# Down-projection of a squared-ReLU MLP: a chunk's seven products chained in PSUM, context products as plain float32

## The chip, the cores and the metric

One core of one Trainium2 chip runs the whole program: two layers of a hybrid backbone on 1,024 latent positions and 256 context positions. TensorE (PE in the profile) multiplies out of SBUF into PSUM, which has eight banks of 128 partitions by 512 float32. VectorE (DVE), ScalarE (ACT) and GpSimd (POOL) do the elementwise work, and SyncE (SP) issues most transfers from and to DRAM. Each engine runs its own instructions in the order of its own queue and waits for the others at semaphores. The metric is the device time of the program in microseconds.

## The reference, cut to what matters

Three token mixers run side by side in each layer, their outputs are projected and added, and then the MLP follows. The change lies in the second product of that MLP, the down-projection.

```python
def sqrelu_mlp(h, w_up, w_down):
    return jnp.square(jax.nn.relu(h @ w_up)) @ w_down

for l in range(DEPTH):                       # DEPTH = 2
    ...
    x = x + ga2 * sqrelu_mlp(modulate(rmsnorm(x, g_norm2[l]), sh2, sc2), w_up[l], w_down[l])
    if not last:                             # the context is needed after layer 0 only
        xc = xc + ga2c * sqrelu_mlp(modulate(rmsnorm(xc, g_norm2[l]), sh2c, sc2c), w_up[l], w_down[l])
return rmsnorm(x, g_final)
```

`x` is 1024 x 1024 in float32, the hidden width is 4096, and `xc` has 256 rows.

## The kernel before

**Number form.** A float32 product is made of three products in the reduced form f32r. Each operand tile is split: ScalarE casts it to its high half (line 142), VectorE or POOL subtracts that from the tile to get the low half (line 143), and `mm3` multiplies high by high, high by low and low by high into one bank (lines 133, 138, 139). Which of the two engines makes a low half is set by a pattern that is stepped through call by call (`lo_`): `DL = "GV"` alternates POOL (G) and VectorE (V) for the down-projection.

**Blocks.** The 1024 positions are two blocks, xT[0] and xT[1], the context is block 2. The up-projection has written the squared ReLU to DRAM as four quadrants (`da`: A11, A12, A21, A22) and for the context as `dac` (layer 0 only). Here the hidden axis is cut into four chunks (`for c in range(NCH)`). Per chunk, four quadrants of A and four of the weight (B11 to B22) come in by `load`, sixteen transfers of 512 KB on SP's queue. Eight combinations of quadrants (`comb`, line 1449) are two 128x1024 operations each, spread over VectorE and POOL by `DA = "GVVV"`. Then come seven block products, P1 to P7, in place of the eight that a plain 2 x 2 multiplication has.

**A product.** `run` (line 1451) goes over four tiles of 128 hidden units. It splits one A and one B tile each and issues `mm3` on four banks: 4 x 4 x 3 = 48 TensorE instructions of 128x512. Split tiles live in a ring of four for A and four or five for B. The eight PSUM banks are six of a pool called "mm" and two of "t"; a product takes four banks, the next one the others.

**After a product.** `put` (line 1416) adds gain x source to the residual tile on VectorE, 128x512 (128x256 for the context); in the last chunk it also squares the new value on ScalarE and adds it to the norm's sum `ss` on POOL or VectorE (lines 1419 to 1422). P1 is copied out of PSUM by ScalarE (line 1518) and put. The sums that the method shares between output quadrants are kept in SBUF (tiles named c, p and wf: `p1`, `u2`, `u3`), and VectorE adds each further product to them out of PSUM (lines 1549, 1560, 1561, 1577, 1585, 1632).

**Context (layer 0).** `ctx_part` (line 1461) is called four times a chunk. The chunk's four context tiles and sixteen weight tiles are split, and 4 x 48 = 192 f32r instructions of 128x256 go to the two banks of "t".

**Order.** The lists `orders` name the sequence of products and context parts, another one for the last chunk. A scheduler that builds the program places instructions of an engine by their expected readiness. In layer 0's last chunk it is steered by `behind`, with the four numbers `AQ`: P7's products after the sixth instruction group go behind the norm's sum (`hk["sum"]`, line 189), P4's behind its broadcast (`hk["R"]`, line 196). `raw` (lines 1187 to 1189) then scales block 0 for layer 1.

## Time and profile before

Three runs took 3148.15, 3155.20 and 3158.84 us.

| | before |
|---|---|
| median of 3 runs | 3155.20 us |
| profiled execution, its own time | 3150.24 us |
| its span | 3148.5 us |
| mean granted clock of TensorE | 0.953 |
| down-projection of layer 0 in the trace | 1269 to 1774 us |
| down-projection of layer 1 in the trace | 2766 to 3126 us |

The page gives busy time for each engine over the whole span. For a change in one stage the views by window say more: the same columns for a stretch of the trace, then the waits of one engine (what it waited for, which engine and tile released it, total, times, longest), and the timeline of single instructions (start, duration, engine, line, output <- inputs, shape). Square brackets behind an instruction give the idle time before it and who ended it. In the views of one line three durations stand as min/median/max in ns.

### The profile page before, as it was taken

To read this page: it belongs to the slowest core of one execution; us is meant where nothing else is said; L and a number is where in the kernel's file an instruction comes from. 1 tells how busy PE (TensorE), PEld (TensorE's weight loads), DVE (VectorE), ACT (ScalarE), POOL (GpSimd) and SP (SyncE) were. 2 spreads that over 40 slices of the span, in tenths; PEclk is the share of its full clock that TensorE was granted. 3 is DMA by queue.
4 is the path that set the end of the run, shared out by engine and by line. 5 is a ranking of instruction groups with operands and counts; after the bars stand their busy time and mean duration, and the time that the engine had idled before them with its cause. 6 is when DMAs were issued, how large, how long until landed. Compare 5 with 4: busy or idle time off the path is not lost. (4 is left out here: it accounts for less than half of the span.)

```text
span 3148.5 us, 41373 instructions
## 1 busy us (share of the span) xinstructions
PE 2880.9 (92%) x14408; PEld 2322.2 (74%) x14408; DVE 2128.3 (68%) x3772; ACT 1202.8 (38%) x2331; POOL 1377.2 (44%) x1111
## 2 busy tenths in 40 slices
PE   7898989989989999889889899899999899989997
PEld 6787866657768888778677688766657688867775
DVE  7769568532687677887888708448523854489998
ACT  3332345342433333333344533235433544333334
POOL 4222234012464343665657433124123665466665
PEclk7999999999989999999999899999999899999998
DMA  6514675133354454432131212356134343352221
GB/s 236 158 60 131 156 167 161 64 100 116 98 196 164 151 162 170 175 102 94 41 107 34 94 54 84 109 133 170 53 118 134 130 139 110 117 201 90 75 76 54
DMA packets 277877, 376.49 MB, mean 120 GB/s; under 512 B 63396, under 2 KB 154468, under 8 KB 276004
## 3 DMA queue, kind: packets, MB, share of 16 engines
q1 hardware_dynamic: 274788, 366.51, 37.2%
q0 software_dynamic: 576, 4.20, 0.4%
q10 hardware_dynamic: 2304, 3.15, 0.3%
q8 instruction: 114, 1.87, 0.2%
q14 instruction: 95, 0.78, 0.1%
HBM read 283.74 MB, written 90.02 MB: 119 GB/s over the span
## 5 line engine op out<-in xcount | busy, mean ns | idle before, releaser
L133 PE MATMUL mm<-A,wr 128*128 128x512 f32 (+1 forms) x840 | 317.0, 380 | 16.2 <-ACT rb L668 9.8
L138 PE MATMUL mm<-A 128*128 128x512 f32 (+1 forms) x636 | 254.3, 401 | 30.0 <-DVE A L143 29.6
L139 PE MATMUL mm<-A 128*128 128x512 f32 (+1 forms) x636 | 246.6, 398 | 23.4 <-DVE A L143 22.7
L143 POOL TENSOR_TENSOR A<-A,A 128x512 fp32r<-128x512 f32 x126 | 217.4, 1737 | 112.9 <-ACT A L142 109.6
L133 PE MATMUL mm<-A 128*128 128x512 f32 (+1 forms) x636 | 230.8, 395 | 10.0 <-ACT A L142 6.2
L142 ACT ACTIVATE A<-A 128x512 fp32r<-128x512 f32 x234 | 139.7, 626 | 256.7 <-PE t L138 109.0
L143 POOL TENSOR_TENSOR wr<-wf,wr 128x512 fp32r<-128x512 f32 x88 | 121.9, 1397 | 249.5 <-ACT wr L142 240.0
L133 PE MATMUL mm<-A,c 128*128 128x256 f32 (+1 forms) x596 | 214.7, 364 | 6.9 <-ACT c L142 3.6
L138 PE MATMUL mm<-A,c 128*128 128x256 f32 (+1 forms) x596 | 216.7, 364 | 3.0 <-DVE A L143 2.1
L139 PE MATMUL mm<-A,c 128*128 128x256 f32 (+1 forms) x596 | 213.8, 361 | 4.7 <-DVE c L143 4.6
L138 PE MATMUL mm<-A,wr 128*128 128x512 f32 (+1 forms) x520 | 194.5, 375 | 8.4 <-DVE A L143 4.1
L143 POOL TENSOR_TENSOR A<-wr,A 128x512 fp32r<-128x512 f32 x100 | 153.0, 1542 | 111.6 <-ACT A L142 111.3
L133 PEld LDWEIGHTS mm<-A,wr 128*128 128x128 f32 x840 | 162.2, 194 | 47.0 <-ACT rb L668 11.1
L139 PE MATMUL mm<-A,wr 128*128 128x512 f32 (+1 forms) x520 | 192.6, 371 | 0.0
L1138 PE MATMUL v<-PT,Vt 128*97 128x512 f32 (+1 forms) x336 | 172.6, 597 | 13.4 <-ACT PT L1137 13.3
L230 DVE SCALAR_TENSOR_TENSOR junk<-wf,t 128x512 bf16<-128x512 f32 x192 | 131.4, 684 | 75.6 <-DMA wf<-in_w_mt 70.8
L142 ACT ACTIVATE A<-wr 128x512 fp32r<-128x512 f32 x195 | 115.8, 622 | 147.9 <-PE t L138 74.4
L1135 PE MATMUL s<-Q,KT 97*128 97x512 f32 (+1 forms) x336 | 172.2, 599 | 0.1
L138 PEld LDWEIGHTS mm<-A 128*128 128x128 f32 x636 | 124.0, 195 | 63.1 <-DVE A L143 36.7
L139 PEld LDWEIGHTS mm<-A 128*128 128x128 f32 x636 | 122.1, 193 | 53.1 <-DVE A L143 28.9
L1137 ACT ACTIVATE PT<-s 128x512 f32<-128x512 f32 (+1 forms) x168 | 98.0, 584 | 148.9 <-PE s L1135 148.6
L143 DVE TENSOR_TENSOR A<-A,A 128x512 fp32r<-128x512 f32 x108 | 126.0, 1183 | 34.5 <-ACT A L142 26.8
(508 smaller groups left out, 8502.2 us busy)
## 6 DMA issues: line engine op xcount, KB each, us to landing
wf<-in_w_mt SPq DMA_DIRECT2D x96, 256.0 KB
x<-in_w_up SPq DMA_DIRECT2D x40, 512.0 KB
r<-in_w_up SPq DMA_DIRECT2D x38, 512.0 KB
A<-in_w_dn SPq DMA_DIRECT2D x36, 512.0 KB
gt<-in_w_mt SPq DMA_DIRECT2D x64, 256.0 KB
da<-wf SPq DMA_DIRECT2D x64, 256.0 KB
da<-p SPq DMA_DIRECT2D x64, 256.0 KB
wr<-da SPq DMA_DIRECT2D x32, 512.0 KB
```

Of the source, the lines that this page charges most:

```text
L133: PE.matmul(ps, lh, rh, start=first, stop=False)
L138: PE.matmul(ps, lh, rl, start=False, stop=False)
L139: PE.matmul(ps, ll, rh, start=False, stop=last)
L142: (hi or S).activation(dst[0], src, AF.Copy) if (hi is None or hi is S) else hi.tensor_copy(dst[0], src)
L143: (lo or G).tensor_tensor(dst[1], src, f32(dst[0]), ALU.subtract)
L230: V.scalar_tensor_tensor(junk, f, 1.0, cb[w], ALU.mult, ALU.mult, accum_out=(ga, modT[l])[kh][:, w, j:j + 1])
L1135: PE.matmul(ps[:, :nq], K[:, tok(kt)], Q[:, :nq], start=True, stop=True)
L1137: S.activation(PT[:, :nq], ps[:, :nq], AF.Exp, scale=scale)
L1138: PE.matmul(po[:97, :nq], Vt[kt // 2][:, kt % 2, h % 2], PT[:, :nq], start=i == 0, stop=i == len(kts) - 1)
```

## The change

- **Chaining.** `mm3` gets a form that opens a bank only when told. One set of four banks, X, takes P1, then P6, P7 and P4 on top of each other; another, Y, takes P2 and later P5, then P3. So the shared sums arise in PSUM. After P6 and P7, ScalarE copies X to SBUF (`u2`, `u3`, lines 1533 and 1560 of the changed kernel), since those intermediate sums are needed for another quadrant while X goes on. VectorE's adds are gone; every result goes through `put`, 28 a chunk in place of 20 (20 out of PSUM, 8 out of `u2` and `u3`).
- **Order.** P1, P2, context, P6, P5, P7, P3, P4; in the last chunk P3 directly behind P5 and the norm's sum and `raw` behind it, then P7, P4. The numbers `AQ` are no longer passed to P7 and P4.
- **Context.** One `ctx_part` a chunk: 64 plain float32 instructions of 128x256 on the unsplit weight tiles and the unsplit context tiles (double buffered), on four banks, with no splits.
- **Engines.** `DA = "V"`: all combinations on VectorE. `DL = "VVVG"`: of four low halves three on VectorE.
- The buffers that the next chunk's quadrants take over are dealt out otherwise (`freed`); in the last chunk of layer 1, P4 goes in two halves of 256 columns on top of X instead of into two bank sets.

Per chunk and engine, counted from the two programs:

| a chunk | before | after |
|---|---|---|
| TensorE 128x512 | 336 f32r | 336 f32r |
| TensorE 128x256, layer 0 | 192 f32r | 64 plain float32 |
| splits, layer 0 / layer 1 | 76 / 56 | 56 / 56 |
| combinations on VectorE / POOL | 12 / 4 | 16 / 0 |
| PSUM adds on VectorE, first three chunks / last | 24 / 8 | 0 |
| updates 128x512 (`put`), first three chunks | 20 | 28 |
| copies on ScalarE | 4 | 8 |
| low halves on POOL, layer 0 / 1 (layer-wide) | 169 / 116 | 80 / 61 |

```diff
-DA = "GVVV"
-DL = "GV"
+DA = "V"
+DL = "VVVG"
...
-    def mm3(ps, lh, ll, rh, rl, first, last, rlast=0):
+    def mm3(ps, lh, ll, rh, rl, first, last, rlast=0, part=False):
+        if part:
+            PE.matmul(ps, lh, rh, start=first, stop=False, skip_group_check=True)
+            PE.matmul(ps, lh, rl, start=False, stop=False, skip_group_check=True)
+            PE.matmul(ps, ll, rh, start=False, stop=last, skip_group_check=True)
+            return
...
-        names = ["A11", "B11", "A21", "A22", "B12", "B22", "S1", "T2", "A12", "B21"]
-        where0 = dict(zip(["A11"] + ["B11", "A12", "B21", "B22"] + ["A21", "A22", "B12", "S1", "T2"], BL))
-        freed = ["A11", "T2", "A21", "B12", "S1", "B11", "A22", "B21", "A12", "B22"]
+        names = ["A11", "B11", "A12", "B21", "A21", "A22", "B12", "B22", "S1", "T2"]
+        freed = ["A11", "T2", "S1", "B11", "A21", "B12", "A12", "B22", "A22", "B21"]
+        where = dict(zip(names, BL))
...
-            A2t = T(big[2], [128, 4, 2, 512], F32R, tag="A2")
+            A2t = T(big[2], [128, 2, 4, 512], tag="A2")
...
+        u2, u3, sc = psl[0:4], psl[4:8], psl[8:12]
...
-            orders = (["P1x", "c11", "P2x", "c21", "c12", "c22", "P6y", "P7x", "P5y", "P4x", "P3y"],
-                      ["P1x", "c11", "P2x", "c21", "c12", "c22", "e2", "P6y", "P5x", "P3y", "e0", "P7x", "P4x", "e1"])
-        else:
-            orders = (["P1x", "P6y", "P2x", "P7y", "P5x", "P4y", "P3x"], ["P1x", "P6y", "P2x", "P5y", "P3x", "e0", "P7x", "P4x"])
-        if ctx_all:
-            where0 = dict(zip(where0, [BL[i] for i in (0, 1, 2, 3, 4, 7, 8, 6, 5, 9)]))
-        where, blk, ca = where0, {}, []
-        p1, u2, u3 = psl[0:4], psl[4:8], psl[8:12]
+        blk = {}
...
-        def run(ps, an, bn, after=None, frm=1):
+        def run(ps, an, bn, fresh=True, done=True, after=None, frm=1):
             for k in range(4):
                 a_ = cAt(blk[an][k])
                 b_ = cBt(blk[bn][k])
                 for j in range(4):
                     sl = slice(128 * j, 128 * j + 128)
                     with behind(after if 4 * k + j >= frm else None):
-                        mm3(ps[j], b_[:, 0, sl], b_[:, 1, sl], a_[:, 0], a_[:, 1], k == 0, k == 3)
-
-        def ctx_part(h, q, lastc):
-            b_ = [cBt(blk[f"B{h + 1}{q + 1}"][k]) for k in range(4)]
-            for j2 in range(2):
-                ps = T(pst, [128, 512], tag="t")
-                for j in range(2):
-                    jj = 2 * j2 + j
-                    o = ps[:, 256 * j:256 * j + 256]
-                    for k in range(4):
-                        sl = slice(128 * jj, 128 * jj + 128)
-                        hs = slice(256 * h, 256 * h + 256)
-                        mm3(o, b_[k][:, 0, sl], b_[k][:, 1, sl], ca[k][:, 0, hs], ca[k][:, 1, hs], k == 0, k == 3)
-                for j in range(2):
-                    jj = 2 * j2 + j
-                    put(2, 4 * q + jj, ps[:, 256 * j:256 * j + 256], (u2 if q else u3)[jj][:, :256] if lastc and h else None)
+                        mm3(ps[j], b_[:, 0, sl], b_[:, 1, sl], a_[:, 0], a_[:, 1], fresh and k == 0, k == 3, part=True)
+
+        def ctx_part(c, lastc):
+            f = A2t[:, c % 2]
+            for i in range(2):
+                nc.sync.dma_start(f[:, 2 * i:2 * i + 2], dac[4 * c + 2 * i:4 * c + 2 * i + 2].rearrange("p q t -> q p t"))
+            ps = banks("Y")
+            for q in range(2):
+                for jj in range(4):
+                    o = ps[2 * q + jj // 2][:, 256 * (jj % 2):256 * (jj % 2) + 256]
+                    for h in range(2):
+                        for k in range(4):
+                            PE.matmul(o, blk[f"B{h + 1}{q + 1}"][k][:, 128 * jj:128 * jj + 128], f[:, k, 256 * h:256 * h + 256],
+                                      start=h + k == 0, stop=h * k == 3)
+                    put(2, 4 * q + jj, o, sc[jj][:, :256] if lastc else None)
...
+        def banks(which):
+            return [mmt() for _ in range(4)] if which == "X" else [mmt(), mmt()] + [T(pst, [128, 512], tag="t") for _ in range(2)]
...
+            load(c, "A12")
+            load(c, "B21")
+            X = banks("X")
+            run(X, "A11", "B11", True, False)
+            for j in range(4):
+                put(0, j, X[j])
+            for n_ in ("B12", "B22", "A21", "A22"):
+                load(c, n_)
+            Y = banks("Y")
+            run(Y, "A12", "B21")
+            for j in range(4):
+                put(0, j, Y[j], sc[j] if lastc else None)
+            if ctx_all:
+                ctx_part(c, lastc)
+            comb("S1", "A21", ALU.add, "A22")
+            comb("A21", "A11", ALU.subtract, "A21")
+            comb("A11", "S1", ALU.subtract, "A11")
+            comb("B11", "B12", ALU.subtract, "B11")
+            comb("T2", "B22", ALU.subtract, "B11")
+            comb("B12", "B22", ALU.subtract, "B12")
+            run(X, "A11", "T2", False, False)
+            if ctx_all and lastc:
+                finish_(2, lastc)
+            for j in range(4):
+                S.copy(u2[j], X[j])
+            comb("A12", "A12", ALU.subtract, "A11")
+            comb("B21", "B21", ALU.subtract, "T2")
+            Y = banks("Y")
+            run(Y, "S1", "B11", True, False)
+            for j in range(4):
+                put(0, 4 + j, u2[j])
+                put(1, 4 + j, Y[j])
+
+            def p3():
+                run(Y, "A12", "B22", False)
+                for j in range(4):
+                    put(0, 4 + j, Y[j], sc[j] if lastc else None)
+
+            if lastc:
+                p3()
+                if last:
+                    finish_(0, lastc)
+                else:
+                    R0 = rstd_bcast(ss[0], 512, D, wk, pst, "t")
+                    hT[0] = h_tile(0)
+                    unit0.append(unit(1, 2, where["A11"]))
+                    nc.sync.dma_start(xs[0], xT[0])
+                    for k in raw(1, 0, 0, hT[0], R0):
+                        pass
+            run(X, "A21", "B12", False, False)
+            for j in range(4):
+                S.copy(u3[j], X[j])
+            for j in range(4):
+                put(1, 4 + j, u3[j], sc[j] if lastc else None, E1)
+            if not lastc:
+                p3()
+            if lastc and last:
...
+                as_ = [cAt(blk["A22"][k]) for k in range(4)]
+                bs_ = [cBt(blk["B21"][k]) for k in range(4)]
+                Rh = [None, None]
+                for th in range(2):
+                    tl = slice(256 * th, 256 * th + 256)
+                    for k, j in [(k, j) for k in range(4) for j in range(4)] if th == 0 else [(k, j) for j in range(4) for k in range(4)]:
+                        sl = slice(128 * j, 128 * j + 128)
+                        mm3(X[j][:, tl], bs_[k][:, 0, sl], bs_[k][:, 1, sl], as_[k][:, 0, tl], as_[k][:, 1, tl], False, k == 3, part=True)
...
+            else:
+                run(X, "A22", "B21", False)
+                if lastc:
+                    unit0.append(unit(1, 6, where["A11"]))
+                for j in range(4):
+                    put(1, j, X[j], sc[j] if lastc else None, V)
```

How the program's order moves, at three places. **First, TensorE in the last chunk of layer 0, the norm's sum of block 0** (t <- ones, ss). Before, the banks mm_14843 to mm_14846 take P7 and mm_14975, mm_14976 already take P4's first products:

```order
L138 MATMUL mm_14975<-A_2294_11588 128x512
L139 MATMUL mm_14975<-A_2294_11588 128x512
L138 MATMUL mm_14976<-A_2294_11588 128x512
L139 MATMUL mm_14976<-A_2294_11588 128x512
L189 MATMUL t_14816<-ones_64,ss_2320_11614 128x1 x4
L133 MATMUL mm_14845<-A_2294_11588 128x512
L138 MATMUL mm_14845<-A_2294_11588 128x512
```

Now mm_13451 to mm_13454 are X:

```order
L134 MATMUL mm_13454<-A_2294_11588 128x512
L135 MATMUL mm_13454<-A_2294_11588 128x512
L136 MATMUL mm_13454<-A_2294_11588 128x512
L194 MATMUL t_13994<-ones_64,ss_2320_11614 128x1 x4
L134 MATMUL mm_13451<-A_2294_11588,c_11605 128x512
L135 MATMUL mm_13451<-A_2294_11588,c_11605 128x512
L136 MATMUL mm_13451<-A_2294_11588,c_11605 128x512
```

The sum stood inside P7; now it stands behind P7's last product, ahead of P4's first.

**Second, the same engine a little later, the broadcast of that norm** (t <- cst, rb_y). Before:

```order
L139 MATMUL mm_14846<-A_2294_11588 128x512
L133 MATMUL mm_14975<-A_2294_11588,c_11605 128x512
L133 MATMUL mm_14976<-A_2294_11588,c_11605 128x512
L196 MATMUL t_14837<-cst_60,rb_y_14823 128x128 x4
L138 MATMUL mm_14975<-A_2294_11588,c_11605 128x512
L139 MATMUL mm_14975<-A_2294_11588,c_11605 128x512
L138 MATMUL mm_14976<-A_2294_11588,c_11605 128x512
```

Now, with the first products of layer 1 (wr as operand) in the last rows:

```order
L136 MATMUL mm_13452<-A_2294_11588 128x512
L134 MATMUL mm_13453<-A_2294_11588 128x512
L201 MATMUL t_14015<-cst_60,rb_y_14001 128x128 x4
L135 MATMUL mm_13453<-A_2294_11588 128x512
L136 MATMUL mm_13453<-A_2294_11588 128x512
L134 MATMUL mm_13454<-A_2294_11588 128x512
L135 MATMUL mm_13454<-A_2294_11588 128x512
L136 MATMUL mm_13454<-A_2294_11588 128x512
L138 MATMUL mm_14261<-A_2401_14020,wr_14022 128x512
L143 MATMUL mm_14261<-A_2401_14020,wr_14022 128x512
```

It stood right behind P7's last product and now stands near P4's end.

**Third, VectorE in a middle chunk of layer 1, where the combinations are made** (128x1024; L1449 before, L1447 now; low halves are L143 and L148, adds L1549, updates L1422). Before:

```order
L1449 TENSOR_TENSOR A_3941_23151<-A_3941_23151,r_3953_23163 128x1024
L1449 TENSOR_TENSOR A_3941_23151<-A_3941_23151 128x1024
L143 TENSOR_TENSOR A_3942_23152<-A_3941_23151,A_3942_23152 128x512
L1549 TENSOR_TENSOR c_23167<-mm_23823,c_23165 128x512
L1549 TENSOR_TENSOR c_23167<-mm_23824,c_23165 128x512
L1549 TENSOR_TENSOR c_23168<-t_23825,c_23166 128x512
L1549 TENSOR_TENSOR c_23168<-t_23826,c_23166 128x512
L143 TENSOR_TENSOR A_3942_23152<-A_3941_23151,A_3942_23152 128x512
L1449 TENSOR_TENSOR A_3941_23151<-A_3941_23151 128x1024
```

Now:

```order
L1447 TENSOR_TENSOR A_3861_22319<-wr_22325,wr_22329 128x1024
L1447 TENSOR_TENSOR A_3861_22319<-wr_22325,A_3861_22319 128x1024
L148 TENSOR_TENSOR A_3862_22320<-wr_22330,A_3862_22320 128x512
L1447 TENSOR_TENSOR r_3874_22332<-wr_22322,r_3874_22332 128x1024
L1447 TENSOR_TENSOR wr_22330<-A_3861_22319,wr_22330 128x1024
L148 TENSOR_TENSOR A_3862_22320<-A_3861_22319,A_3862_22320 128x512
L148 TENSOR_TENSOR A_3862_22320<-wr_22327,A_3862_22320 128x512
L148 TENSOR_TENSOR A_3862_22320<-A_3861_22319,A_3862_22320 128x512
L1447 TENSOR_TENSOR A_3861_22319<-wr_22326,wr_22330 128x1024
L1447 TENSOR_TENSOR A_3861_22319<-wr_22326,A_3861_22319 128x1024
L1422 SCALAR_TENSOR_TENSOR x_3889_22347<-mm_22891,mod_7_67,x_3889_22347 128x512
```

The PSUM adds between the combinations are gone, and more low halves and combinations stand in their place.

More of the change, by code (lines that the diff above doesn't have):

```diff
@@ L1502, in build @@
             blk = {n_: [q[:, i] for q in w_ for i in range(2)] for n_, w_ in where.items()}
-            flip = not ctx_all and c % 2 == 0
             load(c, "A11")
@@ new lines, in build @@
+            run(X, "A21", "B12", False, False)
[6 more added lines that the diff above has]
+            if lastc and last:
+                for k in PK1:
+                    S.activation(xT[1][:, k], xT[1][:, k], AF.Copy, scale=vec[:, V_GF + k:V_GF + k + 1])
+                as_ = [cAt(blk["A22"][k]) for k in range(4)]
[6 more added lines that the diff above has]
+                        mm3(X[j][:, tl], bs_[k][:, 0, sl], bs_[k][:, 1, sl], as_[k][:, 0, tl], as_[k][:, 1, tl], False, k == 3, part=True)
+                    for j in range(4):
+                        xj, sq = xT[1][:, j, tl], u2[j][:, tl]
+                        V.scalar_tensor_tensor(xj, X[j][:, tl], gains(1, j), xj, ALU.mult, ALU.add)
+                        S.activation(sq, xj, AF.Square)
+                        V.tensor_tensor(ss[1][:, tl], ss[1][:, tl], sq, ALU.add)
+                    Rh[th] = rstd_bcast(ss[1][:, tl], 256, D, wk, psm, "mm")
+                    S.copy(u3[1][:, tl], Rh[th][:, :256])
+                for th in range(2):
+                    tl = slice(256 * th, 256 * th + 256)
+                    R = Rh[th]
+                    for k in PO:
+                        o = fin[0][:, 8 + k, tl]
+                        if k in PK1:
+                            G.tensor_tensor(o, xT[1][:, k, tl], u3[1][:, tl], ALU.mult)
+                        else:
+                            with behind("rs" if th == 0 and TB and PO.index(k) >= TB - 1 else None):
+                                V.scalar_tensor_tensor(o, xT[1][:, k, tl], vec[:, V_GF + k:V_GF + k + 1], R[:, :256], ALU.mult, ALU.mult)
+                        (nc.scalar if TQ and PO.index(k) % 2 else nc.sync).dma_start(out[:, k, 512 + 256 * th:768 + 256 * th], o)
+            else:
[4 more added lines that the diff above has]
+                    put(1, j, X[j], sc[j] if lastc else None, V)
+                if lastc:
@@ L1635, in build @@
                     nc.sync.dma_start(xs[1], xT[1])
                     late.append(lambda: [0 for k in raw(1, 0, 1, h=hT[1], R=R1[0])])
-                else:
-                    if o_ == "e0" and not last:
-                        R0 = rstd_bcast(ss[0], 512, D, wk, pst, "t")
-                        hT[0] = h_tile(0)
-                    else:
-                        finish_(int(o_[1]), lastc)
         mp.close()
```

130 lines of the change are left out of this document (3 added, 127 removed).

## The prediction

> **What bounds the kernel now.** I read the page first, then the busy time of each engine over the eight chunks of the down-projection (four of layer 0, four of layer 1), then the waits inside one chunk, then single instructions.
>
> ```profile
> span 3148.5 us, 41373 instructions
> PE 2880.9 (92%) x14408; PEld 2322.2 (74%) x14408; DVE 2128.3 (68%) x3772; ACT 1202.8 (38%) x2331; POOL 1377.2 (44%) x1111
> ...
> core 0: us, PE busy (x) PEld busy (x) DVE busy (x) ACT busy (x) POOL busy (x), PEclk, DMA share, GB/s
> 1269.00:1394.50 125.50, 107.11 (x530) 90.26 (x530) 104.78 (x105) 49.60 (x91) 85.98 (x49) 0.95 0.41 144
> 1394.50:1514.00 119.50, 105.70 (x530) 88.31 (x530) 96.35 (x111) 44.91 (x81) 72.59 (x43) 0.97 0.25 80
> 1514.00:1633.50 119.50, 105.64 (x529) 88.31 (x528) 96.42 (x111) 44.77 (x81) 72.42 (x43) 0.97 0.25 80
> 1633.50:1774.00 140.50, 119.14 (x559) 97.49 (x557) 125.27 (x163) 65.54 (x125) 90.59 (x60) 0.90 0.11 38
> 2766.00:2857.40 91.40, 80.44 (x329) 64.34 (x329) 86.51 (x78) 37.13 (x66) 67.33 (x36) 0.92 0.43 146
> 2857.40:2945.00 87.60, 80.03 (x336) 65.04 (x336) 82.16 (x85) 34.15 (x60) 56.55 (x32) 0.96 0.30 96
> 2945.00:3032.00 87.00, 80.48 (x336) 65.00 (x336) 83.98 (x86) 34.04 (x60) 59.77 (x32) 0.96 0.30 97
> 3032.00:3126.00 94.00, 83.75 (x405) 68.80 (x406) 90.10 (x115) 44.52 (x81) 63.69 (x35) 0.98 0.02 6
> ```
>
> The eight rows sum to 865 us, 27% of the span; only these can move much. The first four are layer 0, the others layer 1. TensorE is the busiest everywhere, but in layer 1 VectorE is busy for 82 to 84 us of an 87 us chunk.
>
> What would a chunk take if TensorE never waited? Products stream at a fixed spacing of starts, here in the timeline:
>
> ```profile
> 1760.18 0.39 PE L133 MATMUL mm<-A 128*128 128x512 f32 x1
> ...
> 1762.00 0.39 PE L139 MATMUL mm<-A 128*128 128x512 f32 x1
> ...
> 1268.57 0.28 PE L139 MATMUL mm<-A,c 128*128 128x256 f32 x1
> ...
> 1268.93 0.28 PE L139 MATMUL mm<-A,c 128*128 128x256 f32 x1
> ```
>
> Eight steps in 1.82 us are 0.2275 each for 512 columns, three in 0.36 are 0.12 for 256. A chunk has 7 x 48 = 336 of the first kind, 76.4 us, and in layer 0 also 192 of the second, 23.0 us. So layer 0's floor is 99.4 and a middle chunk (119.5) loses 20.1; a middle chunk of layer 1 (87.3) loses 10.9. What they wait for in the second chunk of layer 0, then over the whole of layer 1's stage, columns being us, times and the longest:
>
> ```profile
> PE mm L139 <- DVE A L143: 7.0, 4, 4.2
> PE t L139 <- DVE A L143: 3.7, 2, 2.2
> PE t L133 <- DVE x L1416: 1.4, 1, 1.4
> ...
> PE mm L138 <- DVE A L143: 29.6, 14, 4.8
> ```
>
> Nearly all waits end on the low half of an operand (L143) from VectorE. A wait also costs afterwards: the two windows below are a stretch behind a stall and one in full stream (the column after busy is the granted clock).
>
> ```profile
> 1684.00:1689.50 5.50, 5.50 (x26) 0.50 0.01 3
> 1434.00:1443.00 9.00, 8.57 (x67) 1.00 0.36 117
> ```
>
> Why VectorE is late: its two-operand work on SBUF stretches while POOL does the same. First durations (min/median/max in ns) over layer 0's stage, then a stretch of both queues in its second chunk.
>
> ```profile
> L143 DVE TENSOR_TENSOR A<-A,A x76: 674/694/2880, 1268.7 to 1731.5; 128x512 fp32r<-128x512 f32 x76
> L143 POOL TENSOR_TENSOR A<-wr,A x60: 1266/1298/1831, 1276.3 to 1763.1; 128x512 fp32r<-128x512 f32 x60
> L1449 DVE TENSOR_TENSOR wr<-wr,wr x8: 1210/1220/3408, 1291.0 to 1623.9; 128x1024 f32<-128x1024 f32 x8
> L1416 DVE SCALAR_TENSOR_TENSOR x<-mm,mod,x x43: 735/739/750, 1298.7 to 1773.8; 128x512 f32<-128x512 f32 x43
> L1416 DVE SCALAR_TENSOR_TENSOR x<-t,mod,x x66: 467/475/735, 1296.5 to 1742.7; 128x256 f32<-128x256 f32 x64, 128x512 f32<-128x512 f32 x2
> L1561 DVE TENSOR_TENSOR c<-mm,c 128x512 f32<-128x512 f32 x8 | 5.4, 675 | 0.0
> ...
> 1495.20 7.04 POOL L143 TENSOR_TENSOR A<-A,A 128x512 fp32r<-128x512 f32 x4 [0.26 <-ACT A L142]
> ...
> 1499.35 1.77 DVE L1416 SCALAR_TENSOR_TENSOR x<-c,mod,x 128x512 f32<-128x512 f32 x1
> 1501.05 3.42 DVE L143 TENSOR_TENSOR A<-A,A 128x512 fp32r<-128x512 f32 x2
> 1504.38 1.21 DVE L1449 TENSOR_TENSOR wr<-wr,wr 128x1024 f32<-128x1024 f32 x1
> ```
>
> Beside POOL a split or an update from SBUF takes 1.71 to 1.77 on VectorE instead of 0.69 to 0.74, and POOL's own 1.76 instead of 1.30. So each POOL split costs a busy VectorE about 1.05 us. Updates out of PSUM never stretch (735 to 750 over 43).
>
> **The change, part by part.** *Context (layer 0).* 192 products and 20 splits a chunk go, 64 plain float32 products come. Their spacing, from the mixers' stage:
>
> ```profile
> 611.23 0.60 PE L1135 MATMUL s<-Q,KT 97*128 97x256 f32 x2
> 611.67 0.38 PE L758 MATMUL l<-cc,um 128*128 128x128 f32 x2
> ```
>
> The next product starts 0.44 after one of 256 columns, so 64 x 0.44 = 28.2 us: 5.2 more than the 23.0 they replace. Bounds: 0.36, the three f32r passes of today, gives 23.0; 0.60, its whole duration if nothing overlaps, gives 38.4. I take 0.44, the same form of instruction. The floor becomes 76.4 + 28.2 = 104.6. Its operands are not split, so for 28 us TensorE asks nothing of VectorE, which then does the chunk's combinations.
>
> The Trainium skill, "FP8 and Floating Point Precision", section "TensorE Precision Notes", has a rule against this part: true FP32 is four passes through the array. By four passes of the 0.12 above, a product is 0.48 and a chunk 30.7, which would make the forecast 10 us later; the rows' 0.44 lies below that, and no row there is of exactly this shape in a long run.
>
> *Adds and copies.* All 24 PSUM adds of a middle chunk (0.675) leave VectorE, 8 updates more come (28 instead of 20), and ScalarE makes 8 copies instead of 4. ScalarE is busy 34 of 87 us; four more at its present 0.58 hide there.
>
> ```profile
> L1518 ACT COPY c<-mm x28: 563/577/592, 1278.5 to 3055.2; 128x512 f32<-128x512 f32 x28
> ```
>
> *Splits and combinations to VectorE.* In layer 1 a chunk's 56 splits were shared half and half with POOL; now 42 are VectorE's, and all 16 combinations (12 before). Unstretched VectorE work of a chunk: before 28 x 0.69 + 12 x 1.22 + 24 x 0.675 + 20 x 0.74 = 65; measured 83, so POOL's 57 to 60 us cost it 18. After: 42 x 0.69 + 16 x 1.22 + 28 x 0.74 = 69, plus 14 POOL splits, whose cost lies between 18 x (14 x 1.5 / 58) = 7 and 14 x 1.05 = 15. So 76 to 84 of 87: between 7 us freed and 1 us lost a chunk. But the demand is uneven: between P6 and P7 VectorE has combinations, updates and splits together, some 41 + 5 us of work beside 38 us of products, so a wait of about 8 us stays, where 10.9 is lost now. I take -1 a chunk, **-4** for layer 1 (between -28, the 7 us a chunk, and the +8 of the first rival).
>
> The skill's "SBUF — State Buffer", section "Who interferes with whom", says that the port the two engines share is locked for a whole instruction, the loser blocked. By that each POOL split costs up to its 1.30, 18 us a chunk, VectorE reaches 87 and the -4 becomes about 0. The rows above show both engines stretched, which is softer than a full block for one.
>
> In layer 0 the same sum is 44 splits, 16 combinations, 28 updates and 8 of the context (0.475): 74 us, plus 15 to 21 for POOL's: at most 95 in a chunk of 105 or more, with the 28 us of slack of the context. I take 5 of the 20 us of loss as staying (bounds 0 and 15). A middle chunk: 104.6 + 5 = 109.6, **-10**; the first keeps its 6 us of late loads, **-10** too, three together **-30**.
>
> *Last chunk of layer 0.* Today TensorE stands before and inside P7:
>
> ```profile
> 1744.50 1.22 PE L133 MATMUL mm<-A 128*128 128x512 f32 x2 [5.01 <-ACT A L142]
> ...
> 1751.32 1.87 PE L189 MATMUL t<-ones,ss 128*128 128x1 f32 x8 [3.15 <-DVE ss L1422]
> ...
> 1739.30:1757.80 18.50, 9.97 (x26) 0.63 0.32 129
> ```
>
> In these 18.5 us it runs 26 instructions, 6 us at full stream: 12.5 are lost. In the changed order the sum over channels (the ones product) stands after P7's last product instead of inside it, so its lateness no longer holds P7 up; the slow clock behind it goes with it. I take 7 of the 12.5 back: **-17** with the general -10 (bounds -5 and -22).
>
> *Price of it.* The broadcast of the norm of block 0 now stands three products before P4's end, where it stood at P4's beginning; the first tile of layer 1 is behind it.
>
> ```profile
> 1762.68 1.05 PE L196 MATMUL t<-cst,rb_y 128*128 128x128 f32 x8
> ...
> 1766.43 5.34 DVE L1187 SCALAR_TENSOR_TENSOR x<-x,G,t 128x512 f32<-128x512 f32 x8
> ...
> 1767.19 1.38 ACT L1189 ACTIVATE x<-x,mod 128x512 f32<-128x512 f32 x2 [0.68 <-DVE x L1187]
> ```
>
> One step of 0.67 on VectorE, one of 0.69 on ScalarE, a split of 0.6 and one of 0.69 stood under P4; now about 3 us of them are open, and some slow clock: **+4** (0 to +10).
>
> *Joins.* X carries P1, P6, P7, P4 and Y P2, then P5, P3: before a bank is added to again, its copy or update must be done. Between two runs on X lies one on Y of 48 products, 10.9 us, against four copies of 0.58: nothing. In the last chunks P5 goes straight into P3 and P7 into P4; each bank's last product lies about 2 us before the run ends, so the reader has time: nothing to 2 us each. The loads of B12 and B22 move ahead of P2 and the context's into a tile of two halves, all on SP's queue: hidden at a DMA share of 0.25, two products lie between issue and use.
>
> Sum: -30 - 17 + 4 - 4 = -47. The profiled execution took 3150.2 (span 3148.5), so 3103; the runs' median, 3155.2, is 5 above that execution: **3108**.
>
> **Rivals.** (a) *VectorE stays the limit.* Its splits come late as now, only the waits move. For: it is at 76 to 84 of 87 in layer 1. Then layer 1 loses 2 a chunk and layer 0 keeps 13 of its 20 us of loss: four times 104.6 + 13 is only 2 us a chunk better, the last chunk 5 more, the start of layer 1 +4: about -1, time 3154 at its worst, 3131 halfway. (b) *The float32 weight loads are not hidden.* 0.60 per product instead of 0.44: 256 x 0.16 = +41, time 3149. For: one pair of weights serves one product only; against: the 0.44 row. (c) *Slower: the chain serialises.* ScalarE's copies stand in the same queue as its high-half splits; if some eight of them (0.6 each) are ahead of a copy that P7 or P4 waits for, that join costs 5 us plus about 3 at half clock. One such join in each of eight chunks, with (a)'s loss of the gain, gives -1 + 64: 3218; with the gain kept, 3172. It decides once ScalarE runs more than 10.9 us behind, and it is busy only 34 of 87. (d) *All waits go*: layer 0 at its floor, -20, and layer 1 at -28 instead of -4: 3064.
>
> **How the numbers follow.** Forecast 0.57 (its own range 3085 to 3130), (a) 0.22, (b) 0.08, (c) 0.07, (d) 0.06. The range reaches into (d), (a) and (b): 3080 to 3148. A difference under 0.3%, 9.5 us, can't be told from none. Faster: the forecast, (d), and (a) when halfway (0.15), a little of (b): 0.80. The same: the rest of (a) and (b), 0.12. Slower: (c) and a mishap, 0.08.
>
> **What would show it.** Right: a middle chunk of layer 0 near 110 us with context products 0.44 apart; VectorE under 85 us a chunk and POOL under 30; hardly any waits of TensorE on ScalarE's copies; no stall inside P7 of layer 0's last chunk, but 3 to 4 us at layer 1's start; layer 1's chunks 85 to 88. Wrong: context products 0.48 or 0.60 apart; waits on the copies or updates at a run's first product; layer 0's waits on L143's successor still above 8 us a chunk; or splits on VectorE whose median stays at 1.7.

## The result

The changed kernel took 3066.95 us (median of four runs, 3059.47 to 3073.66) against 3157.02 for the kernel before beside it: a ratio of 0.9719, 95% interval 0.9688 to 0.9751. That is 90 us, where 47 were forecast; the time lies below the range. It is nearly the time of the last rival, "all waits go", 3064 us.

The first two lines of the changed kernel's page follow, and the busy time of each engine over the eight chunks (four of layer 0, four of layer 1; columns as in the view of the kernel before):

```profile
span 3061.7 us, 40347 instructions
...
PE 2861.2 (93%) x14152; PEld 2306.0 (75%) x14152; DVE 1982.2 (65%) x3708; ACT 1176.6 (38%) x2283; POOL 1050.2 (34%) x935
```

```profile
core 0: us, PE busy (x) PEld busy (x) DVE busy (x) ACT busy (x) POOL busy (x), PEclk, DMA share, GB/s
1270.40:1380.50 110.10, 105.99 (x467) 88.37 (x466) 80.74 (x96) 38.55 (x70) 21.46 (x15) 0.98 0.51 176
1380.50:1484.30 103.80, 103.80 (x466) 87.39 (x465) 79.13 (x96) 36.68 (x65) 22.20 (x14) 1.00 0.30 92
1484.30:1588.10 103.80, 103.80 (x466) 87.39 (x465) 77.92 (x95) 36.66 (x64) 21.21 (x14) 1.00 0.26 82
1588.10:1706.10 118.00, 109.38 (x489) 90.58 (x487) 94.58 (x130) 52.38 (x103) 53.59 (x41) 0.99 0.12 45
2707.00:2793.00 86.00, 74.66 (x310) 60.34 (x311) 68.52 (x85) 37.06 (x66) 22.26 (x14) 0.92 0.48 162
2793.00:2870.50 77.50, 76.73 (x338) 63.01 (x337) 68.87 (x88) 36.25 (x64) 25.09 (x14) 1.00 0.34 109
2870.50:2948.00 77.50, 76.73 (x338) 63.02 (x337) 66.94 (x88) 36.25 (x64) 28.37 (x14) 1.00 0.34 109
2948.00:3035.50 87.50, 85.47 (x427) 71.83 (x425) 80.66 (x102) 46.88 (x85) 45.18 (x24) 1.00 0.02 7
```

In the middle chunks TensorE is busy for the whole of layer 0's 103.8 us, at the full clock. In layer 1 a steady chunk takes 77.5 us, 1.1 above the 76.4 of its products. VectorE is down from 82 to 84 us a chunk of layer 1 to 67 to 69, POOL from 57 to 60 to 25 to 28.

By stage, from the windows of the two profiled executions (us):

| stage | before | after | difference | forecast |
|---|---|---|---|---|
| up to layer 0's first chunk | 1269.0 | 1270.4 | +1.4 | 0 |
| down-projection of layer 0 | 505.0 | 435.7 | -69.3 | -47 |
| between the two | 992.0 | 1000.9 | +8.9 | +4 |
| down-projection of layer 1 | 360.0 | 328.5 | -31.5 | -4 |
| behind the last product | 22.5 | 26.2 | +3.7 | 0 |
| span | 3148.5 | 3061.7 | -86.8 | -47 |

What TensorE still waits for in the two middle chunks of layer 1 together, all of it:

```profile
PE mm L135 <- POOL A L148: 1.5, 2, 0.8
```

Over the two middle chunks of layer 0 the view of waits is empty. There the forecast had kept 5 us of loss a chunk. The first and last chunks still wait: layer 1's first chunk, 86.0 us long, has 12.5 us of waits for operands (before: 91.4 us, with 9.8 us of waits).

### The profile page after: what moved, and what is told of

Same layout as the page of the kernel before. It is cut to its first block, busy times and chain, and to the rows that moved or that the text cites. A ratio compares the mean times of both kernels' runs of the same rounds, so it can differ in the third digit from the quotient of the medians.

```text
span 3061.7 us, 40347 instructions
## 1 busy us (share of the span) xinstructions
PE 2861.2 (93%) x14152; PEld 2306.0 (75%) x14152; DVE 1982.2 (65%) x3708; ACT 1176.6 (38%) x2283; POOL 1050.2 (34%) x935
## 3 DMA queue, kind: packets, MB, share of 16 engines
q10 hardware_dynamic: 2304, 3.15, 0.3%
## 5 line engine op out<-in xcount | busy, mean ns | idle before, releaser
L148 POOL TENSOR_TENSOR wr<-wf,wr 128x512 fp32r<-128x512 f32 x88 | 122.0, 1396 | 258.8 <-ACT wr L147 199.9
L143 PE MATMUL mm<-A,wr 128*128 128x512 f32 (+1 forms) x520 | 196.1, 378 | 4.6 <-POOL A L148 2.1
L138 PEld LDWEIGHTS mm<-A,wr 128*128 128x128 f32 x840 | 161.5, 193 | 51.5 <-ACT rb L673 12.5
L138 PE MATMUL mm<-A,c 128*128 128x512 f32 (+1 forms) x520 | 184.3, 356 | 15.4 <-ACT c L147 13.3
L1143 PE MATMUL v<-PT,Vt 128*97 128x512 f32 (+1 forms) x336 | 176.7, 610 | 12.5 <-ACT PT L1142 12.5
L143 PE MATMUL mm<-A,c 128*128 128x512 f32 (+1 forms) x520 | 184.9, 356 | 3.1 <-DVE A L148 2.3
L144 PE MATMUL mm<-A,c 128*128 128x512 f32 (+1 forms) x520 | 183.9, 354 | 0.8 <-DVE c L148 0.8
L147 ACT ACTIVATE A<-A 128x512 fp32r<-128x512 f32 x174 | 106.9, 625 | 158.3 <-PE mm L135 85.1
L148 DVE TENSOR_TENSOR A<-wr,A 128x512 fp32r<-128x512 f32 x146 | 128.3, 891 | 42.8 <-ACT A L147 27.7
L135 PEld LDWEIGHTS mm<-A 128*128 128x128 f32 x654 | 123.4, 189 | 39.5 <-DVE A L148 11.9
L134 PEld LDWEIGHTS mm<-A 128*128 128x128 f32 x654 | 122.7, 188 | 31.1 <-ACT A L147 7.0
L136 PEld LDWEIGHTS mm<-A 128*128 128x128 f32 x654 | 123.5, 189 | 24.8 <-DVE A L148 0.7
L138 PE MATMUL mm<-wr,A 128*128 128x256 f32 x464 | 134.0, 289 | 6.6 <-ACT rb L673 4.7
```

What stands on the lines that cost most here:

```text
L134: PE.matmul(ps, lh, rh, start=first, stop=False, skip_group_check=True)
L135: PE.matmul(ps, lh, rl, start=False, stop=False, skip_group_check=True)
L136: PE.matmul(ps, ll, rh, start=False, stop=last, skip_group_check=True)
L138: PE.matmul(ps, lh, rh, start=first, stop=False)
L143: PE.matmul(ps, lh, rl, start=False, stop=False)
L144: PE.matmul(ps, ll, rh, start=False, stop=last)
```

## Experiments

Theory 1: VectorE's total work, stretched by POOL, was the limit, and the adds that left and POOL's share that left both lower it. Theory 2: it was a place, the stretch in which the chunk's combinations, low halves and updates come together. Each ratio below is against runs of the kernel before on the same chip.

### The three parts apart

The chain (with its order), the sharing between VectorE and POOL, and the context can each be undone. The old sharing in the changed kernel:

```diff
-DA = "V"
-DL = "VVVG"
+DA = "GVVV"
+DL = "GV"
```

> The changed kernel with the old sharing between VectorE and POOL (DL = GV, DA = GVVV); chain and plain context stay. Theory 1, POOL's share of the splits and combinations was what made VectorE late: POOL is busy about 55 us a chunk again, VectorE's operations stretch again by some 18 us, a steady chunk of layer 1 is back at 84 to 87 us (now 77.5), and the time is 3067 + 30 to 60 = about 3110. Theory 2, the adds that left VectorE and the chained order were it: layer 1 stays under 80 us a chunk and the time within 15 us of 3067.

And the new sharing alone in the kernel before (the same lines the other way round):

> The kernel before with only the new sharing (DA = V, DL = VVVG); the adds and the f32r context stay. Theory 1: POOL under 30 us a chunk, VectorE's stretch about 6 us a chunk, so 65 + 10 + 5 + 6 = 86 us of work in layer 1 with the adds but little stretch; a chunk of layer 1 falls to 80 to 85 and the time by 20 to 40, to about 3125. Theory 2: VectorE has 15 us more work of its own a chunk, and the time is the same or up to 40 longer (3157 to 3197).

The context alone, in the kernel before:

```diff
-            b_ = [cBt(blk[f"B{h + 1}{q + 1}"][k]) for k in range(4)]
+            b_ = blk[f"B{h + 1}{q + 1}"]
...
-                        mm3(o, b_[k][:, 0, sl], b_[k][:, 1, sl], ca[k][:, 0, hs], ca[k][:, 1, hs], k == 0, k == 3)
+                        PE.matmul(o, b_[k][:, sl], ca[k][:, hs], start=k == 0, stop=k == 3)
...
-                            ca.append(csplit(f[i][:, k], DL, A2t[:, 2 * i + k]))
+                            ca.append(f[i][:, k])
```

> The kernel before with only the context's products as plain float32 on unsplit tiles, in the four parts and the two banks of before. If the context's 20 splits a chunk were what layer 0 waited for, a middle chunk falls from 119.5 to 108 to 112 and the time by 30 to 45. If only the floor counts (4.6 us a chunk more on TensorE, the waits moving on to the next product), the time is 0 to 20 longer. Layer 1 is not touched.

The context as f32r in the changed kernel (in this run each half of a bank is opened by a product of its own while the other half is still being summed, so part of the context's sums is lost; the instructions are the same in number and form):

```diff
+                for h in range(2):
+                    for k in range(4):
+                        b_ = cBt(blk[f"B{h + 1}{q + 1}"][k])
...
+                        for jj in range(4):
...
+                            mm3(o, b_[:, 0, sl], b_[:, 1, sl], ca[k][:, 0, hs], ca[k][:, 1, hs], h + k == 0, h * k == 3, part=True)
```

> The changed kernel with the context as 192 f32r products of split tiles on four banks. If the chain and the sharing alone had freed layer 0, the floor of 99.4 would show: a middle chunk at 100 to 102 and the time 10 to 16 shorter than 3067. If the 20 splits more and the missing quiet 28 us count, a middle chunk takes 108 to 112 and the time is 15 to 35 longer than 3067.

Then the chain alone (both of the edits in the changed kernel, with a bank opened once), and the other two without the chain:

> The changed kernel with the old sharing and with f32r context products: of the change only the chain (with its order) is left. If gains add up, the chain is worth the whole 88 less what the sharing (25) and the context (23) gave alone in the kernel before: 40 us below it. If they need each other, layer 1 stays at 87 a chunk, a middle chunk of layer 0 takes 110 to 118, and the time is 5 to 25 below the kernel before.

> The kernel before with the new sharing and the plain context, without the chain: the adds stay on VectorE. If gains add up, 48 below the kernel before. Layer 1 as with the sharing alone, 87 to 88 a chunk, since VectorE has the adds; in layer 0 a middle chunk at its floor of 104 to 106 if VectorE's total is what counts (its 99 us there, less 20 splits of 0.7, is 85), 108 or more if the order of the adds is.

Measured, with the length of a middle chunk from one copy or update to the same one of the next chunk:

| chain | sharing | context | ratio to before (95%) | layer 0, a chunk | layer 1, a chunk |
|---|---|---|---|---|---|
| - | - | - | 1 | 119.5 | 87.7 |
| - | new | - | 0.9918 (0.9897 to 0.9939) | 111.0 | 86.9 |
| - | - | new | 0.9927 (0.9911 to 0.9942) | 111.9 | 86.8 |
| - | new | new | 0.9910 (0.9881 to 0.9940) | 110.2 | 87.0 |
| new | - | - | 0.9917 (0.9897 to 0.9937) | 109.5 | 87.4 |
| new | - | new | 0.9892 (0.9871 to 0.9914) | 106.0 | 87.4 |
| new | new | - | 0.9753 (0.9733 to 0.9773) | 105.1 | 77.4 |
| new | new | new | 0.9719 (0.9688 to 0.9751) | 103.8 | 77.4 |

Layer 1 shows it most plainly: 87 us without the chain, 87 with the chain and the old sharing, 77.4 with both. Each part alone is worth about 0.8%, two without the other 1%, chain and sharing together 2.5%. For the old sharing the first theory had said 3110 and 84 to 87 us a chunk; 3115.9 and 87.4 were measured. For the new sharing alone it had said 80 to 85, and 87 came out. Here are layer 1's chunks of the kernel before, of the new sharing alone and of the old sharing in the changed kernel, by windows:

```profile
2877.80:2965.50 87.70, 80.28 (x334) 65.11 (x333) 82.26 (x86) 34.17 (x61) 56.93 (x32) 0.95 0.30 97
```

```profile
2843.70:2930.60 86.90, 79.22 (x337) 64.53 (x336) 80.21 (x104) 34.57 (x61) 25.71 (x14) 0.94 0.30 97
```

```profile
2858.10:2945.50 87.40, 78.98 (x337) 63.90 (x336) 77.32 (x68) 36.00 (x66) 55.98 (x33) 0.98 0.30 96
```

The three arrive at about the same VectorE time, 77 to 82 us, by different ways: few operations much stretched (68 in the third row), or many little stretched (104 in the second). Only both parts together bring it to 67 to 69, and only then does the chunk fall to its products. The chain is an edit of many parts: the adds that left VectorE, the new order and the other use of the buffers are in it together, and no run separates them.

In layer 0 VectorE's total is not the limit. With the new sharing and the plain context it is busy for 86.7 of 110.2 us, and the chunk is still 6 us above its products; with the chain, the old sharing and the plain context it is busy for 69.9 of 106.0, 2 us above. The expectation of the former had put 108 us or more down to the order of the adds. In the time of the whole program the gains don't add up either: sharing and context together give 29.7 us, where the two alone sum to 48, and the chain alone gives 27.5, where adding up would leave it 40.

In layer 0 the context is worth 7.6 us a chunk by itself, and 23 us of the time, where 30 to 45 were expected. On top of chain and sharing only 1.3 are left: its floor is 4.6 us higher (76.4 + 27.6 = 104.0 against 99.4 for f32r), and the f32r form in that company loses 5.7, of which 4.7 are waits in the view. Its 105.1 us lie between the two cases of its expectation. That run took 3071.6, the changed kernel 3067 on another chip; the two ratios' intervals overlap, so that little difference isn't settled.

### POOL's share

All low halves on VectorE, and every second one on POOL (all combinations on VectorE in both):

```diff
-DL = "VVVG"
+DL = "V"
```

> The changed kernel with all low halves of the down-projection on VectorE (DL = V), none on POOL. Theory 1, VectorE's total is the limit: its layer-1 chunk is 62 us unstretched plus 14 x 0.60 = 70 and no stretch, below 77, so a chunk stays at 77.4 to 79 and the time is within 10 us of 3067. Theory 2, the dense stretch between P6 and P7 decides: there are now some 45 us of VectorE work beside 38 us of products, 5 to 8 us a chunk are lost, 8 chunks: 20 to 50 us longer.

```diff
-DL = "VVVG"
+DL = "VG"
```

> The changed kernel with every second low half on POOL again (DL = VG), but all combinations on VectorE. Theory 1, only VectorE's total counts: 28 x 0.60 + 16 x 1.13 + 28 x 0.66 = 53 us plus a stretch of 28 x (0.4 to 0.8) = 11 to 22, so 64 to 75, below 77: the chunk stays at 77 to 79. Rival, POOL's own splits come late as soon as both engines stretch each other, whatever VectorE's total: a layer-1 chunk at 82 to 87, the time 25 to 45 longer, like the run with both old patterns (87.4, 86.5).

Without POOL: 0.9697 (0.9668 to 0.9725), 3052.1 us, a steady chunk of layer 1 at 76.7 to 78. The time is 15 us below the 3067 of the changed kernel, better than either theory had it. With every second one on POOL: 0.9813 (0.9793 to 0.9833), 82.4 a chunk in layer 1, 103.8 in layer 0. One chunk of layer 1 of each, in that order:

```profile
2819.50:2896.20 76.70, 76.47 (x337) 62.85 (x337) 71.06 (x101) 35.85 (x65) 0.00 (x0) 1.00 0.33 111
```

```profile
2848.70:2931.10 82.40, 77.47 (x338) 62.81 (x337) 71.99 (x74) 36.33 (x65) 52.15 (x28) 1.00 0.31 104
```

VectorE's busy time is the same, 71 and 72 us, for 101 and for 74 instructions; POOL's help of 28 operations is used up by the stretch. Yet the second takes 5.7 us longer, so VectorE's total is not the whole limit. Late results of POOL, the rival, explain little of it: in that chunk TensorE waits 4.1 us for low halves from VectorE and 0.7 for one from POOL, and VectorE itself waits 1.2 for POOL.

Does POOL cost by the stretch, or because its results come late? A POOL that works for nobody, on top of DL = "V", in the first three chunks of layer 1:

```diff
+        def decoy(src):
+            if last and dk_[0]:
+                dk_[1] += 1
+                G.tensor_tensor(sc[dk_[1] % 4], src, src, ALU.subtract)
...
         def cAt(src):
             nc_[0] += 1
+            decoy(src)
```

> The run with DL = V, and in the first three chunks of layer 1 POOL subtracts each of the 28 A tiles from itself into a scratch tile that nobody reads: 28 operations a chunk, as many as with DL = VG, without any result that is waited for. If POOL costs by stretching VectorE: its 71.4 us grow by 28 x 0.6 = 17, to 85 and more, and a chunk goes from 77 to 86 to 90, the time up by 25 to 40. If POOL costs by its own late results: VectorE is stretched a little, and the chunk stays at 77 to 79.

0.9801 (0.9771 to 0.9832), 3084.2 us, 29.7 above DL = "V" on the same chip. The chunk goes from 77 to 88.6 and 89.8; the third row is the step into the last chunk, nearly without the extra operations:

```profile
2758.20:2846.80 88.60, 81.42 (x342) 64.41 (x341) 88.29 (x99) 36.06 (x64) 53.08 (x32) 0.98 0.28 89
2846.80:2936.60 89.80, 81.53 (x338) 64.59 (x336) 86.73 (x101) 36.10 (x66) 47.26 (x29) 0.96 0.29 94
2936.60:3016.00 79.40, 77.27 (x338) 62.70 (x336) 76.12 (x101) 39.16 (x72) 7.92 (x6) 1.00 0.27 86
```

The view of the line that issues them (durations as min/median/max in ns) names nobody behind "who waited":

```profile
L1407 POOL TENSOR_TENSOR c<-wr x18: 1035/1484/6710, 2740.1 to 2935.6; 128x512 f32<-128x512 f32 x18
...
who waited for it (us, times):
busy tenths in 40 slices 0000000000000000000000000000000000065400
```

With the same 101 instructions VectorE is busy for 87 to 88 us instead of 71: 16 to 17 us of stretch by 28 operations, 0.6 each, as this run's expectation had it. The stretch alone is enough to bring back the 87 us of the kernel before.

### A place or a total

Eight more updates of VectorE a chunk into a scratch tile, in layer 1, on top of DL = "V"; first after P1 and P2, then after P5 and P3:

```diff
             for j in range(4):
                 put(0, j, X[j])
+                if last and not lastc:
+                    V.scalar_tensor_tensor(sc[j], X[j], gains(0, j), xT[0][:, j], ALU.mult, ALU.add)
```

> The run with DL = V (no POOL at all), and in the first three chunks of layer 1 eight more VectorE updates of 0.66 us, after P1 and P2 into a scratch tile, that change no result: 5.3 us a chunk more, put where VectorE was busy without a break (P4 to P6 of the next chunk). Theory 2, that stretch is the limit: a steady chunk goes from 77 to 81 to 83. Theory 1, only VectorE's total counts: 71.4 + 5.3 = 76.7 is still below 77, so 77 to 78.

> The same eight updates, but after P5 and P3, where VectorE had idle time. Theory 2: nothing, 77 to 78 a chunk. Theory 1: the same as with the updates in the dense place, 77 to 78 for both. If both take 81 to 83, neither holds and the updates' reading of the banks is what costs.

Each of these two kernels ran once only. One chunk of each:

```profile
2826.50:2907.50 81.00, 76.97 (x338) 62.83 (x336) 76.22 (x109) 35.64 (x65) 0.00 (x0) 1.00 0.32 104
```

```profile
2843.60:2924.90 81.30, 78.69 (x340) 64.32 (x338) 77.39 (x111) 36.15 (x66) 0.00 (x0) 0.98 0.35 112
```

Both places cost the same: 81.0 and 82.8 for the first, 81.3 and 79.6 for the second. Neither theory said that. The total is 76 to 77, below the floor, and should have cost nothing by theory 1; the place should have decided by theory 2. The third explanation in the expectation, that the updates' reading of the banks costs, holds in part in the first run: there TensorE also waits for an added update (L1516) that still reads its bank. In the second run all its waits are for low halves from VectorE. Here are the waits over the same two chunks, first run, then second:

```profile
PE mm L134 <- ACT A L147: 3.6, 2, 1.8
PE mm L135 <- DVE A L148: 2.0, 3, 1.1
PE mm L134 <- DVE c L1516: 1.6, 1, 1.6
```

```profile
PE mm L135 <- DVE A L148: 6.3, 5, 2.0
```

What stands: at 71 us or less without POOL, VectorE costs TensorE nothing; from 72 (stretched in places) to 76 on it does, in a chunk of 77. A likely reason, which no run shows by itself: work added where VectorE had idle time takes away the lead with which it enters the busy part. Where exactly the limit lies, and by what rule, stays open.

### The join of the layers, and the end

The two hints of the kernel before, handed to P7 and P4 again:

```diff
-            run(X, "A21", "B12", False, False)
+            q_ = lastc and not last
+            run(X, "A21", "B12", False, False, "sum" if q_ else None, AQ[0])
...
-                run(X, "A22", "B21", False)
+                run(X, "A22", "B21", False, True, "R" if lastc else None, AQ[1])
```

> The changed kernel with the two hints of the kernel before handed to P7 and P4 of layer 0's last chunk: the norm's sum inside P7 and its broadcast early in P4 again. If the late broadcast is what the start of layer 1 pays for (about 5 us from the end of P4 to the first common landmark), the time falls by 3 to 6; if the sum then stalls P7 as in the kernel before (2.8 to 3.2 us and slow clock behind it), it is 0 to 5 longer.

0.9738 (0.9719 to 0.9757), 3068.1 us: no gain and no loss. But two amounts moved. From layer 0's last product start to layer 1's first it is 992.1 us instead of 1001.1, and layer 0's stage takes 446.1 instead of 435.5 by the same measure. The sum waits for POOL's squares in both: in the changed kernel behind P7, and with the hints, longer, inside P7:

```profile
1693.31 1.05 PE L194 MATMUL t<-ones,ss 128*128 128x1 f32 x8 [2.78 <-POOL ss L1428]
```

```profile
1696.41 1.87 PE L194 MATMUL t<-ones,ss 128*128 128x1 f32 x8 [8.72 <-POOL ss L1428]
```

Of the 9.0 us saved between the layers 7.4 lie between P4's last product and a broadcast well inside layer 1 (at 1850.98 in the changed kernel, 1857.66 here), so they do come from the join; the early broadcast costs as much again by an earlier wait. With the squares on VectorE and DL = "V" too:

```diff
-                    put(0, 4 + j, Y[j], sc[j] if lastc else None)
+                    put(0, 4 + j, Y[j], sc[j] if lastc else None, E0)
```

> DL = V, the hints, and in P3 of the last chunks the squares summed on the engine that the pattern SE names (VectorE in layer 0) instead of POOL, so that the sum is ready sooner. Expected: the 8 us or so of layer 1 that DL = V gave, and 4 to 8 at the join of the layers: 3045 to 3055 in this comparison, the fastest of all. If the sum still comes late, no better than DL = V alone.

0.9734 (0.9704 to 0.9764), 3062.3 us: not the fastest. The sum still waits 6.7 us, now for VectorE, and the end behind the last product grows to 29.1 us. A miss.

That end is 3.7 us longer in the changed kernel than before. VectorE stands there for POOL's sum of squares:

```profile
3043.33 2.77 DVE L1580 TENSOR_TENSOR ss<-ss,c 128x256 f32<-128x256 f32 x8 [5.55 <-POOL ss L1428]
```

```diff
-                put(1, 4 + j, u3[j], sc[j] if lastc else None, E1)
+                put(1, 4 + j, u3[j], sc[j] if lastc else None, V)
```

> DL = V, and in the last chunk of layer 1 the squares of the updates out of u3 are summed on VectorE instead of POOL. If POOL's sum is what the end waits for, the stretch behind the last product goes from 26.3 to about 22 to 23 us and the time is 3 to 4 shorter than with DL = V; if POOL's scaling of block 0 only hands its place on, the stretch stays at 26.

On top of DL = "V": 0.9676 (0.9647 to 0.9705), 3050.2 us; the end takes 24.3 instead of 26.2. The wait was real, but only 1.9 of its 5.55 us were to be had, less than the 3 to 4 expected; the median is below that of DL = "V", but the intervals overlap.

### The better version

The changed kernel and DL = "V" once more, five runs of each on one chip:

> The changed kernel once more, beside the next run on the same chip: 0.972 of the kernel before.

> DL = V once more. If POOL's 14 low halves a chunk still cost VectorE something that TensorE feels (0.4 us a chunk in layer 1, and a first chunk that starts slowly), it is 5 to 12 us faster than the changed kernel; if not, within 3 us.

0.9749 (0.9722 to 0.9775) and 0.9707 (0.9680 to 0.9733): 3060.82 to 3072.61 against 3051.68 to 3056.71 us, medians 15.7 apart, and no run of the one reaches the other. Without POOL the down-projection is faster than either kernel. By the stages of the two profiled executions layer 0 has 9.3 us less, the stretch between 5.2, layer 1 only 2.8: not where the expectation looked for it. The 5.2 lie in the mixers of layer 1, which the edit doesn't touch; why they are shorter is not shown. In layer 0's last chunk the sum's wait for POOL is gone from the view of waits.

## Why the prediction was wrong, by its own steps

**The direction and the place were right; two terms were far too small.** Of the missing 40 us of span, 27.5 lie in layer 1 and 22 in layer 0; the stretch between the layers and the end took 8.6 back and the start 1.4.

**Layer 1, "-4 (between -28 and +8)": measured -31.5.** The step that failed is VectorE's time after the change, "76 to 84 of 87"; it is 67 to 69. Three errors went the same way. First, the counts were multiplied by durations, and consecutive operations of VectorE overlap. Three low halves in a row, and three updates, in the changed kernel:

```profile
2886.49 1.88 DVE L148 TENSOR_TENSOR A<-wr,A 128x512 fp32r<-128x512 f32 x3
...
2892.26 2.06 DVE L1422 SCALAR_TENSOR_TENSOR x<-mm,mod,x 128x512 f32<-128x512 f32 x3
```

With a first one of 0.68, 1.88 is 0.60 for each further; 2.06 with 0.74 is 0.66. So the unstretched work is 42 x 0.60 + 16 x 1.13 + 28 x 0.66 = 62, not 69 (1.13 is 1.21 less the same overlap). The run with DL = "V" bears the spacings out: they give 70 for it, and 71 were measured. Second, for the kernel before the same sum gives 58, so that POOL's stretch there was 25 us of 83, not 18: the prize for taking POOL away was larger than it looked. Third, the stretch that stays was taken as 7 to 15 us; 67 to 69 less 62 is 5 to 7, some 0.4 for each of POOL's 14 operations. The "1.05 us" was read at a place where both engines worked without a break.

**"But the demand is uneven ... a wait of about 8 us stays": wrong.** In the changed kernel VectorE works without a break for 34 us (2876 to 2910), and TensorE waits 0.8 there. That VectorE enters the busy part with a lead is my reading of it. The added updates show that there is a limit: eight of them cost 3 to 6 us a chunk. The sign "layer 1's chunks 85 to 88" failed with this step: the steady chunks took 77.5.

**Layer 0, "5 of the 20 us of loss as staying": measured 0.** The forecast named the bounds 0 and 15 and chose 5 without a row. It had itself VectorE at "at most 95 in a chunk of 105"; measured are 78 to 79 of 103.8, with the same errors in it (and 44 low halves in place of the 42 that VectorE makes). All four chunks came out about 5.5 us shorter than forecast (110.1, 103.8, 103.8 and 118.0 against 115.5, 109.5, 109.5 and 123.5).

**Last chunk of layer 0, "no stall inside P7": right, but the stall moved.** The 5.01 us ahead of P7 are gone; the sum still waits 2.78 behind P7, where it waited 3.15 inside.

**Context, 0.44 a product: right.** A product shows as two instructions:

```profile
1409.98 0.59 PE L1468 MATMUL t<-A,A 128*128 128x256 f32 x2
1410.41 1.46 PE L1468 MATMUL mm<-A,wr 128*128 128x256 f32 x6
```

The next product starts 0.43 later; 64 make 27.6 us. The Trainium skill's four passes ("FP8 and Floating Point Precision", "TensorE Precision Notes") at 0.12 each would be 0.48; the measurement decides for 0.43, 3.6 times the f32r pass. The price was sized right, but what it buys is small beside the chain and the new sharing.

**Joins, "nothing to 2 us each": right in the middle chunks, not in two others.** No wait of TensorE on a copy of ScalarE stands in any of the middle chunks. But in layer 0's first chunk the context's products wait for an update, and in its last chunk the products on a bank of "t" wait for the scaling of the context, which reads its broadcast out of such a bank. The forecast has neither:

```profile
1296.77 8.68 PE L1468 MATMUL mm<-A,A 128*128 128x256 f32 x32 [4.11 <-DVE x L1422]
...
1662.20 0.77 PE L134 MATMUL t<-A 128*128 128x512 f32 x1 [4.03 <-DVE x L1192]
```

**Price at the start of layer 1, "+4 (0 to +10)": right at the place it was meant for.** The table's 8.9 holds more than that place. Here are P4's last product and a broadcast well inside layer 1, before and then in the changed kernel:

```profile
1772.44 0.39 PE L139 MATMUL mm<-A 128*128 128x512 f32 x1
...
1913.47 0.71 PE L196 MATMUL t<-cst,rb_y 128*128 128x128 f32 x4 [2.19 <-POOL rb_y L178]
```

```profile
1705.89 0.39 PE L136 MATMUL mm<-A 128*128 128x512 f32 x1
...
1850.98 0.71 PE L201 MATMUL t<-cst,rb_y 128*128 128x128 f32 x4 [2.31 <-POOL rb_y L183]
```

From the one to the other it is 141.0 us before and 145.1 after: 4.1 more, where 4 were forecast. Some 3.6 come later, up to layer 1's first product of the down-projection (852.4 and 856.0), in code that the edit doesn't touch; two executions of DL = "V" differ there by 3.3, so no cause can be given. The rest of the 8.9 is the table's limit of 1774, which lies behind six products of layer 1.

**The end, not in the sum: +3.7.** P7's updates now come late into the norm's sum, on POOL, and VectorE's sum of P4's squares waits for them. The forecast has no term for it, and 1.9 of the 3.7 went when VectorE added them.

**Rivals.** (d), "all waits go", had 0.06 and came out for the middle chunks. That its 3064 lies so near the time is partly luck: its 28 us in layer 1 were four times a bound on VectorE's time, while the middle chunks gained 10 each and the first and last 5.4 and 6.5, with waits left in them; and the losses between the layers and at the end, which it had too small, took back more than it had missed. (a), VectorE stays the limit, is what happens in layer 1 with either the chain or the sharing alone: 87 us a chunk. For the whole change it did not come, because both its savings on VectorE, 14 us of adds and 20 us of stretch, fall on an engine that stood at the limit, and neither shows until it is under that.

## What to carry to other kernels

When an engine is near its limit, add its work up by spacing of starts and not by durations, once for the kernel before as well; what is left over there is contention, and it says what moving the other engine's work away is worth. Two savings on such an engine can each be worth little and together a lot, so an edit that looks useless alone is to be tried with the other. An engine that helps over a shared resource may cost as much as it does: here POOL's 28 low halves a chunk were worth less than nothing.

## What the runs showed of the hardware that had not been expected

POOL's cost to VectorE doesn't depend on its results: 28 subtractions a chunk that nobody waited for lengthened VectorE's busy time from 71 to 87 us and the chunk from 77 to 89. The stretch per POOL operation was not a constant: 0.4 us with 14 a chunk, 0.6 with 28, 0.8 in the kernel before (25 us by 32, of which four are twice as large). By the Trainium skill's "SBUF — State Buffer", "Who interferes with whom", the loser stands for the whole instruction of the other, which is 1.30 us for a low half here; the runs show a third to two thirds of that on average, so the forecast that VectorE would reach 87 us by this rule did not come true. This doesn't speak against the section: where both engines worked without a break, each took 1.71 to 1.77 us an operation, and by my estimate the 0.60 and 1.30 of the two alone add up to 1.9, about what taking turns would give. Updates whose source is in PSUM were never stretched (at most 0.75 us, in the kernel before and in the runs with POOL), as the section has it for operations with one SBUF input; their two inputs here are one in PSUM and one in SBUF.
